# A decoder layer with three mixing branches: value weights split early, gate steps shared by two mLSTM units, three mLSTM operations on GpSimd

## Chip, cores and metric

One NeuronCore of a Trainium2 chip runs the whole layer. The metric is the device time in microseconds of one execution; lower is better. The kernel before takes 2176.12 us, the median of three runs (2176.08 to 2177.18).

## What is computed

The layer normalises x (1024 tokens of 1024 features), projects it, and runs three branches side by side: an mLSTM matrix memory (4 heads, keys of 128, values of 256, chunks of 128 tokens), causal differential attention, and cross attention into 256 memory tokens. Learned gates merge them; an MLP follows. The part that matters here, cut from the reference:

```
h = rms_norm(x, norm_mix_g[l])
mq, mk, mv, mi, mf, mo, dq, dk, dv, cq = jnp.split(h @ w_in[l], split_idx, axis=-1)
qk = jax.nn.silu(causal_depthwise_conv(jnp.concatenate([mq, mk], axis=-1), conv_w[l], conv_b[l]))
hm = mlstm_chunkwise(...)
y_m = jax.nn.sigmoid(mo) * rms_norm(hm, m_norm_g[l])
# mlstm_chunkwise, per chunk:
w_intra = jnp.exp(logd - m_loc[..., None])          # masked by causality
w_inter = jnp.exp(inter - m_loc)
s = jnp.einsum('bhjd,bhsd->bhjs', qq, kk) * w_intra
num = jnp.einsum('bhjs,bhsv->bhjv', s, vv) + w_inter[..., None] * jnp.einsum('bhjd,bhdv->bhjv', qq, C)
C_new = decay[..., None, None] * C + jnp.einsum('bhs,bhsd,bhsv->bhdv', w_s, kk, vv)
g_m, g_d, g_c = jnp.split(jax.nn.sigmoid(h @ w_gate[l] + b_gate[l]), N_BRANCH, axis=-1)
```

## The kernel before

Every fp32 matrix operand is held as two parts: ACT casts it to the high part (a CAST in the profile) and DVE subtracts that from the source to get the low part (a TENSOR_TENSOR or SCALAR_TENSOR_TENSOR from two inputs). `split`, `split2` and `splits` (L104 to L121, L247) do this, and `mm3` (L123) makes a product of two such operands by three matmuls. Nearly all of TensorE's matmuls have line L93.

Within a stage the code sets the order of the work by hand. `weave` (L608) runs a stream of steps, one product of an operand pair (three matmuls) at each, and issues items of other work when the stream has come to their position p. Instructions issued through `InOrder` (L58) or `pin` (L88), TensorE's among them, stay in that order on their engine; the others, GpSimd's in `branch_m` among them, are placed by the scheduler. Each engine works through its own queue in order; SP issues the loads and stores. L68 is the helper behind `InOrder`, so that many instructions have this line and are told apart by their tiles.

Three stages matter, one after the other.

`branch_c` (L440) is cross attention. Its stream has 64 query steps and then 32 gate steps (p from 65 to 96). Gate steps come from `gate_steps` (L579): a matrix of `h @ w_gate`, at the end of each 8 steps an activation on ACT into the tile gt and a store of gt by SP (L604, "gates<-gt"). The items are the scores, the probabilities (`probs` L502: RECIPROCAL and then the product cpe, on GpSimd for seven tiles and on DVE for the eighth), their transposes cpT and the value products sc<-cpT,mv.

`m_first` (L701) begins the mLSTM branch. `pieces` (L716) loads the first head's value weights (wmv3, tiles raw) and splits them into eight w tiles of 128x264; then eight value tiles (24 matmuls each) are made with them, of which va is the split result, and 32 gate steps follow. Beside this, at positions p of these 96 steps, `whole` (L773) makes four products hb on GpSimd (128x2048 each), `sums` (L778) four sums of each on DVE, and `low` (L785) splits them into sx; `raw`, `wsum` and `wsp` (L745 to L765) load, sum and split the output-gate weights into wo. Then come seven units of products of sums and weight sums, seven at a time, each in a PSUM bank of its own (bk). Two of the banks are those that the gate tiles use.

`branch_m` (L917) has eight units, head 3, 2, 1, 0 times the two halves of the sequence. Per unit the stream makes q and k (`f_tile`, two tiles of 8 steps) and, except for head 3, the values (`v_tile`); after the first unit's q and k it has 32 gate steps. `conv` (L972) makes the convolution and SiLU (tiles pre, cv, cth) and the operands qh and kh. The items of a unit are `inter` (L1002: wib, loaded, times q, gives qp), `decays` (L1035: ngb, loaded, plus the causal mask, then four exponentials on ACT), `krows` (transposes of k, scaled into ks), `scores` (k times q, times ngb, split into mpT), four times `chunk` (L1070: products with mpT, ks, qp and the state; the state C and its split Ch go on to the next chunk), and three times `final` (L1110: the output hS is scaled, transposed and gated). Their positions stand in the table at L1169 to L1184: kt for krows, st for scores, ch for the chunks, fi for the finals.

Of the kernel before, what the change touches and what calls it, by code (L numbers as in the profile page):

```python
# [10 lines left out]
F32 = mybir.dt.float32  # L11
F32R = mybir.dt.float32r
# [5 lines left out]
P = 128  # L18
# [54 lines left out]
class Layer:  # L73
# [366 lines left out]
    def branch_c(self, pool):  # L440
# [102 lines left out]
        for k in range(NK):  # L543
            add(41 + 2 * k + k // 2, self.gate_load)
        b4 = ((58, 64), (66, 69), (70, 74), (75, 79)), ((84, 87), (87, 90), (90, 93), (93, 96))
# [155 lines left out]
    def m_first(self, gp, wrp, sxp, wop, evp, pbk):  # L701
# [12 lines left out]
        wqk, wv = self.wqk, self.wv = {}, {}  # L714

        def pieces(d, hd, src, n, wait):  # L716

            d[hd] = []
            rq = []
            k = 0  # L720
            while k < NK or rq:
                while k < NK and len(rq) < wait:
                    raw = wrp.tile([P, 528], F32, tag="wraw", name=self.name("raw"))
                    S.dma_start(raw[:, 0 : 2 * n].rearrange("p (k n) -> p k n", k=2), src[:, k : k + 2, :])
                    rq.append(raw)
                    k += 2
                raw = rq.pop(0)
                for i in range(2):
                    t = self.wp.tile([P, 2, 264], F32R, tag="w", name=self.name("w"))
                    self.split2(t[:, 0, 0:n], t[:, 1, 0:n], raw[:, i * n : (i + 1) * n])  # L730
                    d[hd].append((t[:, 0, 0:n], t[:, 1, 0:n]))
                    yield

        for _ in pieces(wv, 3, a["wmv3"], 264, 4):
            pass
# [75 lines left out]
        def at(n, f):  # L811
            todo.setdefault(n, []).append(f)
# [13 lines left out]
        at(78, lambda: (wsum(2), sums(2)))  # L826
        at(82, lambda: (wsp(), raw(), wsum(3)))
        at(84, lambda: low(2))
        at(90, lambda: (wsp(), raw()))
# [24 lines left out]
        bank = [bank[0], b0[0], bank[1], b0[1]] + bank[2:]  # L854
# [3 lines left out]
        qk = pieces(wqk, 3, a["wmqk"][3], 256, 4)  # L858
# [58 lines left out]
    def branch_m(self, pool, tail):  # L917
# [84 lines left out]
        def inter(hd, hf, part=2):  # L1002
# [11 lines left out]
            V.tensor_mul(wib, wib, h["cv"][0])  # L1014
# [20 lines left out]
        def decays(hd, hf, part=2):  # L1035
# [10 lines left out]
            V.tensor_add(  # L1046
# [63 lines left out]
        def final(hd, hf, m):  # L1110
            h = H[hd, hf]
            hS, ss = h["hS"], h["ss"]
            if m == 0:
                for i in range(4):
                    self.pin(V.tensor_scalar_mul(hS[:, i], hS[:, i], ss[:, 4 + i : 5 + i]))
                return
# [19 lines left out]
        def stream():  # L1136
            for n in range(8):
# [7 lines left out]
                if n == 0:  # L1145
                    for _ in range(32):
                        next(filler)
                        yield
# [18 lines left out]
        for n in range(8):  # L1167
            hd, hf = heads[n // 2], n % 2
            if n == 0:  # L1169
# [854 lines left out]
    def run(self):  # L2024
        tc, nc = self.tc, self.nc
        with ExitStack() as ctx:
# [23 lines left out]
            with ExitStack() as c1:  # L2050
# [7 lines left out]
                with ExitStack() as c2:  # L2058
                    E2 = lambda *x, **k: c2.enter_context(tc.tile_pool(*x, **k))
                    kv = E2(name="kv", bufs=1)  # L2060
                    self.wp = E2(name="wp", bufs=4, side="right")
                    self.rp = E2(name="rp", bufs=5, side="right")
# [7 lines left out]
                    with tc.tile_pool(name="rpc", bufs=2) as self.grp, tc.tile_pool(name="pc", bufs=2) as pc, tc.tile_pool(name="pc1", bufs=1) as pc1, tc.tile_pool(name="pc3", bufs=3) as pc3, tc.tile_pool(name="pc4", bufs=8) as pc4, tc.tile_pool(name="wpc", bufs=8) as self.gwp:  # L2070
# [5 lines left out]
                        self.branch_c(T2())  # L2076
                with ExitStack() as c3:
                    E3 = lambda *x, **k: c3.enter_context(tc.tile_pool(*x, **k))
                    R3 = lambda n, k, **kk: Ring([E3(name=f"{n}{i}", bufs=1, **kk) for i in range(k)])
                    gm = E3(name="gm", bufs=1, side="right")  # L2080
                    self.wp = R3("wpa", 8, side="right")
                    with ExitStack() as c4:
                        E4 = lambda *x, **k: c4.enter_context(tc.tile_pool(*x, **k))
                        R4 = lambda n, k, **kk: Ring([E4(name=f"{n}{i}", bufs=1, **kk) for i in range(k)])
                        wrp = R4("wrm", 4, side="right")
# [4 lines left out]
                        self.m_first(gm, wrp, sxp, wop, evp, pbk)  # L2090
# [108 lines left out]
```

## Time and profile before

| | |
|---|---|
| median of three runs | 2176.12 us |
| the profiled execution, its time | 2179.45 us |
| its span, first to last instruction | 2177.7 us |
| busy: TensorE, DVE, ACT, GpSimd | 2145.4, 1444.7, 972.2, 620.0 us |
| share of the span | 99%, 66%, 45%, 28% |
| mean granted clock of TensorE | 0.995 |

Cross attention ends near 172 us of the span, `m_first` runs from there to 361.6, `branch_m` from there to about 625. PE is TensorE, POOL is GpSimd, PEld the weight loads of TensorE. A timeline joins instructions of one kind that follow each other; the time in square brackets is how long the engine stood before them, and on what. In the windows, PEclk is the granted clock of TensorE, where 1.00 is 2.4 GHz and 0.50 is 1.2 GHz. The end of a matmul is modelled, so the starts are what can be relied on. Spans on GpSimd are rough.

### The profile page before, as it was taken

Reading aid. Unit: us, or ns where it says so; the run is one execution under the profiler, and the core shown is the slowest. Engines: PE = TensorE matmul, PEld = TensorE weight load, DVE = VectorE, ACT = ScalarE, POOL = GpSimd, SP = SyncE. Lnnn points to the kernel's source line nnn. Section 1 sums busy time; section 2 is a strip of 40 time slices with the busy share of each in tenths; the row PEclk is TensorE's granted clock in tenths of the full one; section 3 lists DMA queues with packets and bytes.
Section 4 is the critical chain, followed back from the end, with each engine's and each line's share of the span. In section 5 each row is a group of like instructions: output and inputs, shape, how many; then the busy total and the mean of one; then the engine's idle time right before and its main releaser. Section 6 shows DMA issues by size and latency. Waiting matters only on the chain. (4 is left out here: it accounts for less than half of the span.)

```text
span 2177.7 us, 30462 instructions
## 1 busy us (share of the span) xinstructions
PE 2145.4 (99%) x11042; PEld 1850.7 (85%) x11042; DVE 1444.7 (66%) x2620; ACT 972.2 (45%) x1933; POOL 620.0 (28%) x833
## 2 busy tenths in 40 slices
PE   8998999999999999999999999999999999999998
PEld 7888788899989999999988888888778888788887
DVE  6446745767625888888864333553588778876678
ACT  7543334555534666666654120223433333543331
POOL 2213641000001111111100002202566666564444
PEclk9999999999999999999999999999999999999999
DMA  7022236331131111111125443435534454744442
GB/s 254 20 88 76 84 108 198 100 95 54 45 121 47 44 49 42 45 49 40 37 85 164 155 160 111 136 116 184 164 131 173 141 208 145 283 161 151 160 159 97
DMA packets 116100, 254.96 MB, mean 117 GB/s; under 512 B 11721, under 2 KB 20206, under 8 KB 113902
## 3 DMA queue, kind: packets, MB, share of 16 engines
q1 hardware_dynamic: 113646, 240.44, 33.8%
q10 hardware_dynamic: 2304, 12.58, 1.4%
q8 instruction: 87, 1.43, 0.3%
q14 instruction: 63, 0.52, 0.1%
HBM read 177.45 MB, written 71.34 MB: 114 GB/s over the span
## 5 line engine op out<-in xcount | busy, mean ns | idle before, releaser
L93 PE MATMUL mm<-w,hT 128*128 128x384 f32 (+3 forms) x2496 | 458.3, 331 | 6.7 <-DVE w L68 5.0
L68 POOL TENSOR_TENSOR wraw<-wraw 128x128 f32<-128x128 f32 x608 | 385.2, 658 | 231.1 <-DMA wraw<-in_wdown 122.2
L93 PEld LDWEIGHTS mm<-w,hT 128*128 128x128 f32 x2496 | 392.5, 190 | 19.5 <-DVE w L68 5.4
L93 PE MATMUL p<-xo,wo 128*128 128x512 f32 x1344 | 307.4, 390 | 3.4 <-DVE u L68 1.7
L93 PE MATMUL p<-xd,wo 128*128 128x512 f32 x1344 | 306.1, 389 | 0.8 <-DVE acc_xt L68 0.5
L93 PEld LDWEIGHTS p<-xo,wo 128*128 128x128 f32 x1344 | 251.6, 188 | 58.0 <-DVE u L68 3.0
L93 PEld LDWEIGHTS p<-xd,wo 128*128 128x128 f32 x1344 | 251.9, 188 | 54.8 <-DVE acc_xt L68 0.9
L93 PE MATMUL mm<-hT,w 128*128 128x512 f32 x1152 | 287.2, 397 | 0.2
L68 DVE TENSOR_TENSOR wo<-wraw,wo 128x896 fp32r<-128x896 f32 x153 | 186.0, 1225 | 140.3 <-ACT wo L68 138.4
L68 ACT CAST wo<-wraw 128x896 fp32r<-128x896 f32 x153 | 142.7, 943 | 297.9 <-POOL wraw L68 125.6
L93 PE MATMUL mm<-kt,w 128*128 128x512 f32 x1152 | 261.3, 389 | 0.0
L93 PEld LDWEIGHTS mm<-kt,w 128*128 128x128 f32 x1152 | 216.2, 188 | 44.9
L93 PEld LDWEIGHTS mm<-hT,w 128*128 128x128 f32 x1152 | 209.6, 188 | 42.6 <-ACT pre L980 0.5
L68 ACT ACTIVATE dpe<-sc,dst,drr 128x256 f32<-128x256 f32 (+7 forms) x128 | 106.6, 833 | 73.6 <-DVE dst L68 72.6
L117 ACT CAST w<-raw 128x256 fp32r<-128x256 f32 (+1 forms) x80 | 51.4, 662 | 126.4 <-PE mm L93 101.1
L68 DVE CUSTOM_DVE_ANT_0 sc<-sc,tmask 128x256 f32<-128x256 f32 (+7 forms) x128 | 97.2, 759 | 5.3 <-PE sc L93 4.3
L68 DVE TENSOR_TENSOR w<-raw,w 128x384 fp32r<-128x384 f32 (+3 forms) x128 | 76.6, 615 | 34.1 <-ACT w L68 34.0
L118 DVE TENSOR_TENSOR w<-raw,w 128x256 fp32r<-128x256 f32 (+1 forms) x80 | 61.7, 786 | 39.7 <-ACT w L117 39.6
L141 POOL TENSOR_SCALAR dso<-dso 128x4 f32<-128x4 f32 x16 | 3.4, 210 | 295.4 <-DVE dso L68 295.4
L93 PE MATMUL bk<-sx,wo 128*128 128x512 f32 x336 | 85.6, 390 | 1.5 <-ACT gt L68 1.5
L93 PE MATMUL mm<-mh,w 128*128 128x512 f32 x256 | 79.0, 389 | 0.0
L93 PEld LDWEIGHTS bk<-sx,wo 128*128 128x128 f32 x336 | 63.0, 188 | 15.0 <-ACT gt L68 1.9
(344 smaller groups left out, 3224.4 us busy)
## 6 DMA issues: line engine op xcount, KB each, us to landing
wraw<-in_wup SPq DMA_DIRECT2D x64, 256.0 KB, 3.3
r_d<-xts SPq DMA_DIRECT2D x16, 1024.0 KB, 4.3
xd<-r_d SPq DMA_DIRECT2D x16, 1024.0 KB, 5.4
wraw<-in_wdown SPq DMA_DIRECT2D x64, 256.0 KB, 5.3
raw<-in_wd SPq DMA_DIRECT2D x32, 384.0 KB, 3.2
kraw<-y SPq DMA_DIRECT2D x24, 512.0 KB, 4.6
gl<-gates SPq DMA_DIRECT2D x48, 256.0 KB, 2.7
r_d<-rq ACTq DMA_DIRECT2D x16, 768.0 KB, 3.3
```

Of the source, the lines that this page charges most:

```text
L68: return self.tc.keep_in_program_order(f(*a, **k))
L93: self.pin(self.nc.tensor.matmul(out, l, r, start=start, stop=stop))
L117: nc.scalar.copy(hi, src)
L118: nc.vector.tensor_sub(lo, src, f32(hi))
L141: g.tensor_scalar(r, ss, 1.0 / width, EPS, op0=ALU.mult, op1=ALU.add)
```

## The change

It has three parts. **Early splits:** at p = 72 of `branch_c` two pools that are no longer used are closed and those of the value weights opened; the loads of wmv3 start there, and its eight splits are issued at p = 78 to 92. The pool of the gate tiles and gate bias in `m_first` moves to the other side of the memory, so that the gate bias load now comes behind the last cross-attention matmuls. **Gate steps and positions:** of the 32 gate steps after the first unit's q and k, 16 stay there and 16 come after the second unit's, and the positions of the units' items are new; in `m_first` sums(2), low(2) and the third wsp come earlier, and the second of the two banks that gate tiles use takes the seventh product instead of the fourth. **GpSimd:** in `branch_m` the mask addition on ngb, the product wib, and the scaling of hS (four DVE operations of 128x256 before, now one product of 128x1024) run on GpSimd.

The diff, cut to its core:

```diff
-    def branch_c(self, pool):
+    def branch_c(self, pool, room):
...
+        def begin():
+            room()
+            self.early = self.pieces(self.wv, 3, self.a["wmv3"], 264, 4)
+
+        add(72, begin)
+        for p in (78, 80, 82, 84, 86, 88, 90, 92):
+            add(p, lambda: next(self.early))
...
-        for _ in pieces(wv, 3, a["wmv3"], 264, 4):
+        for _ in self.early:
             pass
...
-        at(78, lambda: (wsum(2), sums(2)))
+        at(76, lambda: (wsum(2), sums(2)))
         at(82, lambda: (wsp(), raw(), wsum(3)))
-        at(84, lambda: low(2))
-        at(90, lambda: (wsp(), raw()))
+        at(80, lambda: low(2))
+        at(88, lambda: (wsp(), raw()))
...
-        bank = [bank[0], b0[0], bank[1], b0[1]] + bank[2:]
+        bank = [bank[0], b0[0]] + bank[1:5] + [b0[1], bank[5]]
...
-            V.tensor_mul(wib, wib, h["cv"][0])
+            G.tensor_mul(wib, wib, h["cv"][0])
...
-            V.tensor_add(
+            nc.gpsimd.tensor_add(
                 ngb.rearrange("p (t j) -> p t j", t=4), ngb.rearrange("p (t j) -> p t j", t=4),
                 self.tmaskT.unsqueeze(1).broadcast_to([P, 4, P]),
             )
...
             if m == 0:
-                for i in range(4):
-                    self.pin(V.tensor_scalar_mul(hS[:, i], hS[:, i], ss[:, 4 + i : 5 + i]))
+                self.pin(G.tensor_mul(hS, hS, ss[:, 4:8].unsqueeze(2).broadcast_to([P, 4, 256])))
                 return
...
-                if n == 0:
-                    for _ in range(32):
+                if n < 2:
+                    for _ in range(16):
                         next(filler)
                         yield
...
-                kt, st, ch, fi = 32, 35, (39, 43, 47, 51), (62, 72, 78)
+                kt, st, ch, fi = 29, 34, (38, 42, 46, 50), (55, 63, 68)
             elif n == 1:
-                add(62, inter, hd, hf)
-                add(70, decays, hd, hf)
-                kt, st, ch, fi = 77, 82, (85, 91, 98, 104), (112, 118, 123)
+                add(50, inter, hd, hf)
+                add(56, decays, hd, hf)
+                kt, st, ch, fi = 60, 66, (72, 77, 82, 88), (97, 107, 113)
...
-                ch, fi = (e + 7, e + 11, e + 15, e + 21), (e + 33, e + 44, e + 50)
+                ch, fi = (e + 7, e + 11, e + 15, e + 21), (e + 32, e + 45, e + 51)
...
+                    def room():
+                        cr.close()
+                        R = lambda c, n, k: Ring([c.enter_context(tc.tile_pool(name=f"{n}{i}", bufs=1, side="right")) for i in range(k)])
+                        self.wp = R(cw, "wpa", 8)
+                        self.wrp = R(cq, "wrm", 4)
...
-                    gm = E3(name="gm", bufs=1, side="right")
-                    self.wp = R3("wpa", 8, side="right")
+                    c3.push(cw)
+                    gm = E3(name="gm", bufs=1)
```

How the instructions move is shown at three places. The first is DVE in cross attention, round the eighth cpe product (cpT are low parts of transposed probabilities, yc copies of the branch's output). Before:

```order
L68 TENSOR_TENSOR cpT_1372<-tp_1367,cpT_1372 128x512
L68 TENSOR_TENSOR cpT_1383<-tp_1378,cpT_1383 128x512
L68 RECIPROCAL cmx_1314<-cmx_1314 128x4
L68 TENSOR_TENSOR cpe_1340<-cpe_1340,cmx_1314 128x1024
L68 COPY yc_1410<-sc_1397 128x512
L68 COPY yc_1413<-sc_1397 128x512
```

Now:

```order
L68 TENSOR_TENSOR cpT_1410<-tp_1405,cpT_1410 128x512
L68 TENSOR_TENSOR cpT_1421<-tp_1416,cpT_1421 128x512
L68 TENSOR_TENSOR w_1438<-raw_1430,w_1438 128x264
L68 RECIPROCAL cmx_1314<-cmx_1314 128x4
L68 TENSOR_TENSOR cpe_1378<-cpe_1378,cmx_1314 128x1024
L68 COPY yc_1459<-sc_1446 128x512
L68 COPY yc_1462<-sc_1446 128x512
L68 TENSOR_TENSOR w_1471<-raw_1430,w_1471 128x264
L68 TENSOR_TENSOR w_1481<-raw_1432,w_1481 128x264
L68 TENSOR_TENSOR w_1490<-raw_1432,w_1490 128x264
```

The subtraction that makes the low part of the first value-weight tile, w_1438, stands ahead of the RECIPROCAL and the cpe product, and three more follow the copies yc.

The second is ACT at the end of the gate steps of `m_first` (gt are the gate activations after 8, 16, 24 and 32 steps; sx_2143 and sx_2121 are the third sum's high parts in the two kernels, wo the output-gate weights). Before:

```order
L68 CAST sx_2056<-hb_1764 128x4x512
L68 ACTIVATE gt_2071<-mm_2039,dv 128x512
L68 CAST wo_2087<-wraw_2021 128x7x128
L68 ACTIVATE gt_2118<-mm_2080,dv 128x512
L68 CAST wo_2128<-wraw_2023 128x7x128
L68 CAST sx_2143<-hb_2013 128x4x512
L68 ACTIVATE gt_2158<-mm_2121,dv 128x512
L68 CAST wo_2168<-wraw_2025 128x7x128
L68 ACTIVATE gt_2191<-mm_2161,dv 128x512
```

Now:

```order
L68 CAST sx_2056<-hb_1764 128x4x512
L68 ACTIVATE gt_2071<-mm_2039,dv 128x512
L68 CAST wo_2087<-wraw_2021 128x7x128
L68 ACTIVATE gt_2118<-mm_2080,dv 128x512
L68 CAST sx_2121<-hb_2013 128x4x512
L68 CAST wo_2131<-wraw_2023 128x7x128
L68 ACTIVATE gt_2158<-mm_2124,dv 128x512
L68 CAST wo_2161<-wraw_2025 128x7x128
L68 ACTIVATE gt_2191<-mm_2166,dv 128x512
```

The cast of sx stands ahead of the second wo cast instead of behind it, and the third gt behind both; on SP the order of loads and stores is as before, a load of wraw ahead of each store of gt, and that ahead of the third store refills the buffer that the second wo is split from.

The third is the start of `branch_m`, first on ACT (cth, qh and qp are of the first unit's q, kh and ks of its k, gt are gate activations, the first of which frees the bank of the tile after next). Before:

```order
L991 ACTIVATE cth_3382<-cv_3377 128x512
L1053 ACTIVATE ngb_3328<-ngb_3328,g_col 128x128 x4
L120 ACTIVATE qh_3385<-cv_3377 128x512
L120 ACTIVATE qp_3410<-wib_3330 128x512
L603 ACTIVATE gt_3504<-mm_3471,dv 128x512
L991 ACTIVATE cth_3433<-cv_3428 128x512
L117 CAST kh_3436<-cv_3428 128x512
L603 ACTIVATE gt_3540<-mm_3507,dv 128x512
```

Now:

```order
L1062 ACTIVATE ngb_3328<-ngb_3328,g_col 128x128 x4
L1000 ACTIVATE cth_3382<-cv_3377 128x512
L120 ACTIVATE qh_3385<-cv_3377 128x512
L1000 ACTIVATE cth_3433<-cv_3428 128x512
L120 ACTIVATE qp_3410<-wib_3330 128x512
L612 ACTIVATE gt_3504<-mm_3471,dv 128x512
L117 CAST kh_3436<-cv_3428 128x512
L253 ACTIVATE ks_3533<-tp_3528,g_col 128x128 x4
L612 ACTIVATE gt_3554<-mm_3507,dv 128x512
```

The exponentials of ngb stand ahead of the activation of q, and qp and the first gt behind that of k. On GpSimd the moved operations come in this order, where ngb_3328 and wib_3330 are of the first unit, ngb_3804 and wib_3770 of the second, ngb_4184 of the third (before, GpSimd had only the hss operations here):

```order
L1055 TENSOR_TENSOR ngb_3328<-ngb_3328,tmaskT 128x512
L1055 TENSOR_TENSOR ngb_3804<-ngb_3804,tmaskT 128x512
L1023 TENSOR_TENSOR wib_3330<-wib_3330,cv_3377 128x512
L1055 TENSOR_TENSOR ngb_4184<-ngb_4184,tmaskT 128x512
L1023 TENSOR_TENSOR wib_3770<-wib_3770,cv_3629 128x512
L141 TENSOR_SCALAR hss_3600<-hss_3600 128x4
L142 TENSOR_TENSOR hss_3600<-hss_3600,mhalf 128x4
L1123 TENSOR_TENSOR hS_3599<-hS_3599,hss_3600 128x1024
```

The second unit's mask addition stands between the first unit's mask addition and its product wib, which on DVE came before it.

## Rows read from the trace of the kernel before

**Rows 1.** The page, section 1: busy us (share of the span) x instructions of each engine.
```profile
PE 2145.4 (99%) x11042; PEld 1850.7 (85%) x11042; DVE 1444.7 (66%) x2620; ACT 972.2 (45%) x1933; POOL 620.0 (28%) x833
```

**Rows 2.** The list of TensorE's waits: line waited for: us in total, times, longest.
```profile
PE bk L93 <- ACT gt L68: 1.7, 2, 1.5
...
PE sc L93 <- DVE Ch L118: 0.6, 2, 0.4
```

**Rows 3.** Timeline of TensorE, 170 to 204: start, us, what, [idle before <-releaser].
```profile
169.66 2.26 PE L93 MATMUL sc<-cpT,mv 128*128 128x512 f32 x9
...
178.93 24.58 PE L93 MATMUL mm<-w,hT 128*128 128x264 f32 x188 [4.03 <-DVE w L68]
...
182.81 20.70 PE L93 MATMUL mm<-w,hT 128*128 128x264 f32 x168
203.35 0.86 PE L93 MATMUL mm<-hT,gws 128*128 128x512 f32 x3
```

**Rows 4.** Timeline of DVE, 169 to 184.
```profile
173.22 7.71 DVE L68 TENSOR_TENSOR w<-raw,w 128x264 fp32r<-128x264 f32 x8
```

**Rows 5.** Timelines of GpSimd, DVE and TensorE in cross attention, 130 to 153.
```profile
135.68 1.89 POOL L507 TENSOR_TENSOR cpe<-cpe,cmx 128x1024 f32<-128x1024 f32 x1 [9.30 <-DVE cmx L68]
...
142.07 1.22 DVE L68 TENSOR_TENSOR cpe<-cpe,cmx 128x1024 f32<-128x1024 f32 x1
...
148.77 0.60 PE L96 MATMUL tp<-ident,cpe 128*128 128x128 f32 x4
```

**Rows 6.** Timeline of TensorE, 224 to 233.
```profile
229.34 1.65 PE L93 MATMUL bk<-sx,wo 128*128 128x512 f32 x6 [1.50 <-ACT gt L68]
```

**Rows 7.** Timelines of ACT and DVE, 213 to 232.
```profile
225.46 0.67 ACT L68 ACTIVATE gt<-mm,dv 128x512 f32<-128x512 f32 x1
226.04 0.93 ACT L68 CAST wo<-wraw 128x896 fp32r<-128x896 f32 x1
228.59 0.69 ACT L68 ACTIVATE gt<-mm,dv 128x512 f32<-128x512 f32 x1 [1.63 <-DMA gates<-gt]
...
227.79 1.34 DVE L68 TENSOR_TENSOR wo<-wraw,wo 128x896 fp32r<-128x896 f32 x1
```

**Rows 8.** Timelines of DVE and TensorE, 413 to 439.
```profile
414.72 1.14 DVE L1115 TENSOR_SCALAR hS<-hS,hss 128x256 f32<-128x256 f32 x4
...
430.57 0.50 PE L93 MATMUL sc<-va,mpT 128*128 128x258 f32 x2 [1.60 <-ACT mpT L117]
431.74 0.58 PE L93 MATMUL sc<-va,mpT 128*128 128x258 f32 x1 [0.66 <-DVE mpT L118]
...
432.76 4.04 PE L93 MATMUL mm<-w,hT 128*128 128x256 f32 x18
```

**Rows 9.** Windows: length, PE, PEld, DVE, ACT, POOL busy (x), PEclk, DMA.
```profile
42.00:48.00 6.00, 4.06 (x19) 3.26 (x20) 6.00 (x10) 4.55 (x8) 0.00 (x0) 0.79 0.50 150
413.00:432.00 19.00, 16.27 (x91) 13.58 (x90) 19.00 (x42) 11.70 (x27) 0.00 (x0) 0.98 0.38 126
431.00:438.00 7.00, 6.34 (x30) 6.26 (x30) 4.54 (x13) 3.38 (x9) 0.00 (x0) 0.51 0.26 76
```

**Rows 10.** Timelines of TensorE and DVE, 360 to 394.
```profile
361.56 22.81 PE L93 MATMUL mm<-hT,w 128*128 128x512 f32 x96
...
384.56 2.32 PE L93 MATMUL mm<-hT,w 128*128 128x512 f32 x9
...
382.08 0.69 DVE L1046 TENSOR_TENSOR ngb<-ngb,tmaskT 128x512 f32<-128x512 f32 x1 [0.17 <-DMA ngb<-g_dng]
```

**Rows 11.** Groups by line on GpSimd: shapes xcount | busy us, mean ns | idle.
```profile
L68 POOL TENSOR_TENSOR xts<-rq 128x512 f32<-128x512 f32 x15 | 19.6, 1305 | 60.2 <-ACT rq L68 60.2
...
L507 POOL TENSOR_TENSOR cpe<-cpe,cmx 128x1024 f32<-128x1024 f32 x7 | 13.5, 1933 | 15.5 <-DVE cmx L68 15.5
```

**Rows 12.** Timelines of GpSimd and DVE, 203 to 216.
```profile
205.20 4.62 POOL L68 TENSOR_TENSOR hb<-hT 128x2048 f32<-128x2048 f32 x1 [26.62 <-DVE sx L68]
...
205.76 6.20 DVE L68 TENSOR_TENSOR sx<-hb,sx 128x2048 fp32r<-128x2048 f32 x1 [0.17 <-ACT sx L68]
```

More of the change, by code (lines that the diff above doesn't have):

```diff
@@ L544, in branch_c @@
             add(41 + 2 * k + k // 2, self.gate_load)
+        self.wqk, self.wv = {}, {}
+        def begin():
[4 more added lines that the diff above has]
+            add(p, lambda: next(self.early))
         b4 = ((58, 64), (66, 69), (70, 74), (75, 79)), ((84, 87), (87, 90), (90, 93), (93, 96))
@@ L699, in m_gates2, with pieces, m_first @@
         self.pin(self.nc.scalar.copy(self.gcol, ps2[:, 0 : 3 * W]))
-    def m_first(self, gp, wrp, sxp, wop, evp, pbk):
+    def pieces(self, d, hd, src, n, wait):
+        d[hd] = []
+        rq, wrp = [], self.wrp
+        k = 0
+        while k < NK or rq:
+            while k < NK and len(rq) < wait:
+                raw = wrp.tile([P, 528], F32, tag="wraw", name=self.name("raw"))
+                self.S.dma_start(raw[:, 0 : 2 * n].rearrange("p (k n) -> p k n", k=2), src[:, k : k + 2, :])
+                rq.append(raw)
+                k += 2
+            raw = rq.pop(0)
+            for i in range(2):
+                t = self.wp.tile([P, 2, 264], F32R, tag="w", name=self.name("w"))
+                self.split2(t[:, 0, 0:n], t[:, 1, 0:n], raw[:, i * n : (i + 1) * n])
+                d[hd].append((t[:, 0, 0:n], t[:, 1, 0:n]))
+                yield
+    def m_first(self, gp, sxp, wop, evp, pbk):
         nc, a = self.nc, self.a
@@ L713, in m_first @@
         va = self.va = [gp.tile([P, 2, 258], F32R, name=f"va{t}") for t in range(8)]
[L714 to L732, printed above, removed]
-        for _ in pieces(wv, 3, a["wmv3"], 264, 4):
+        wqk, wv, wrp = self.wqk, self.wv, self.wrp
+        for _ in self.early:
             pass
@@ L857, in m_first @@
         at(1, lambda: low(3))
-        qk = pieces(wqk, 3, a["wmqk"][3], 256, 4)
+        qk = self.pieces(wqk, 3, a["wmqk"][3], 256, 4)
         for i, n in enumerate((-5, -5, -4, -4, -3, -3, -2, -2)):
@@ L2060, in run @@
                     kv = E2(name="kv", bufs=1)
-                    self.wp = E2(name="wp", bufs=4, side="right")
-                    self.rp = E2(name="rp", bufs=5, side="right")
+                    cr = ExitStack()
+                    self.wp = cr.enter_context(tc.tile_pool(name="wp", bufs=4, side="right"))
+                    self.rp = cr.enter_context(tc.tile_pool(name="rp", bufs=5, side="right"))
+                    cw, cq = ExitStack(), ExitStack()
+                    def room():
[3 more added lines that the diff above has]
+                        self.wrp = R(cq, "wrm", 4)
                     with tc.tile_pool(name="ptmp", bufs=1) as tmp0, tc.tile_pool(name="ptmp2", bufs=2) as tmp, tc.tile_pool(name="ptmp8", bufs=8) as tmp8:
@@ L2075, in run @@
                         self.gpool = T2()
-                        self.branch_c(T2())
+                        self.branch_c(T2(), room)
                 with ExitStack() as c3:
@@ L2084, in run @@
                         R4 = lambda n, k, **kk: Ring([E4(name=f"{n}{i}", bufs=1, **kk) for i in range(k)])
-                        wrp = R4("wrm", 4, side="right")
+                        c4.push(cq)
                         sxp = [E4(name=f"sxp{i}", bufs=1) for i in range(4)]
@@ L2089, in run @@
                         pbk = E4(name="pbk", bufs=1, space=PSUM)
-                        self.m_first(gm, wrp, sxp, wop, evp, pbk)
+                        self.m_first(gm, sxp, wop, evp, pbk)
                     self.psc = E1(name="psc2", bufs=2, space=PSUM)
```

## Prediction, made before the changed kernel was run

> **What bounds the kernel now.** I read the page's busy times first: TensorE is busy 99% of the span [rows 1]. No other engine can be the bound over the whole program, and the change removes no matmul, so all it can win is time in which TensorE stands, and time in which it runs at the lower clock after standing. Next I read the list of TensorE's waits, to see which of them lie where the change works, then the timelines round each, and last the clock of those stretches. Three places come out.
>
> At the start of the first mLSTM stage, `m_first` (place A), the last matmuls of cross attention end at 169.66 + 2.26 = 171.92 us and the gate tiles begin at 203.35 [rows 3]. In between lie eight value tiles of 24 matmuls. From 182.81 on they run undisturbed, 168 matmuls in 203.35 - 182.81 = 20.54 us, 122.3 ns each [rows 3], so all 192 need 23.5 us. They got 31.4. Some 8.0 us are lost, 4.03 of them in one wait at 178.93. The reader should see why: the eight subtractions that make the low parts of the value weights occupy DVE for 7.71 us from 173.22 on [rows 4].
>
> At the switch from gate tiles to output-gate products (place B) TensorE waits twice for a gate activation, 1.7 us together, the longer one at 229.34 [rows 2, 6].
>
> In the second mLSTM unit (place C) it waits 1.60 and 0.66 us for the two halves of mpT, because DVE has no idle time at all from 413 to 432 [rows 8, 9]. Then it runs at half clock, 1.2 GHz of 2.4, from 431 to 438 [rows 9]: 18 matmuls of 256 columns from 432.76 on take 4.04 us [rows 8], 224 ns each against some 122 of 264 columns at place A, so somewhat over 40% of those 7 us, some 3.0, are lost too. C costs 5.3 us.
>
> **The change, part by part.** Durations are from one profiled execution of 2179.45 us (span 2177.7, the rest lies around it); it is 0.15% over the median of 2176.12. I add up differences in that execution and take them off the median.
>
> *Early splits: -8.0 us.* The sixteen casts and subtractions, with their four loads, move into cross attention, onto ACT, DVE and SP. Eight subtractions at about 0.4 us find room on DVE there. One spot is tight. The two products hb for the later sums no longer wait for buffers of cross attention, so GpSimd should run them right after its last cpe product, which ended at 135.68 + 1.89 = 137.57 [rows 5]. At about 4.6 us each [rows 12] they hold GpSimd until about 146.8. The first moved subtraction now stands on DVE ahead of the RECIPROCAL and the cpe product, which needs 1.22 us [rows 5]. If GpSimd holds it until 146.8, then 0.42 + 0.17 + 1.22 end at 148.6, and TensorE takes the result at 148.77 [rows 5]: hidden, with 0.2 to spare. Without that cover one transpose waits up to 2 us. The gate bias load, now behind the last cross-attention matmuls on SP with the gate-weight loads after it, ends well before the first tile's results need it two tiles later. Bounds -6 (a late cpe) to -8.0; I take -8.0, since the row of the cpe leaves room.
>
> *First-stage order: +1.4 us.* On ACT the cast of sx now comes ahead of the second wo cast, and the third gate activation behind both. It ran at 225.46, right after sx, and the wo cast that followed took 0.93 [rows 7]; the activation moves by about 0.84, and the wait of 0.2 behind it becomes about 1.05. The product that uses the last bank moves from fourth to seventh place, from which three places of 0.71 us are gained (96 matmuls in 22.81 us are 0.71 for three [rows 10]). But the last gate activation also shares its one buffer with the third: it started at 228.59, when that store had landed, 2.46 us after the third activation's end at 226.13 [rows 7]. In the changed order SP holds a weight load ahead of that store, and the load waits for the second wo's low part, which now ends at 227.79 + 1.34 = 229.13 [rows 7]. So: store at 229.5, landing about 231.9, activation done at 232.6. The seventh product could start at 227.05 + 5 x 0.71 = 230.6. It waits 2.0. Together 3.05 against 1.7. Bounds: -0.5, if the load gets out of the way, +2.5 with a late landing.
>
> *Sixteen gate steps before and sixteen after the first half-head: -4.8 us.* The second unit's convolutions now run in the first unit's stretch, and 16 steps of 0.71 us stand ahead of its key rows. The scores no longer have convolutions, qh and wib of two units between them and mpT on DVE. I take 5.3 off and leave 0.5 for the closer spacing; bounds -5.3 and -3.
>
> *Start of the mLSTM units: +1.5 us.* Mask and inter product move to GpSimd, which runs them in the order mask 0, mask 1, inter 0. On DVE mask 1 sat at 382.08, having waited for its transfer [rows 10], and inter 0 had been done before it. Now inter 0 stands behind that transfer. With 1.3 us for a product of this shape on GpSimd [rows 11]: 382.1 + 1.3 + 1.3 = 384.7. On ACT qp follows, and the gate activation behind qp frees the bank for the next tile: 0.67 each, as the gate takes it [rows 7], so 386.0. That tile could start at 384.56 [rows 10]. TensorE waits 1.5 (a wait of 0.6 for the key transposes lies inside it). Bounds 0, if the transfer lands earlier, and 2.5, with a DVE subtraction of 0.7 ahead of each GpSimd product.
>
> *GpSimd in the other units: +0.3 us.* Per unit DVE loses 0.69 + 0.69 (one of them in [rows 10]) + 1.14 for the output scaling [rows 8], and GpSimd gains 1.3 + 1.3 + 1.93 = 4.5, by its products of 128x512 and 128x1024 [rows 11]. The rows show what this can do: a DVE subtraction started at 205.76, 0.56 us into a GpSimd product of 4.62, and took 6.20, which is until 2.1 us after that product's end [rows 12]. In the units the only chain with no slack is the state's low part Ch, 0.6 us in two waits [rows 2]. A relieved DVE may save these; one hS product of 1.93 that blocks Ch at both places costs 3.9. Bounds -0.6 and +3.9; I take +0.3, nearer to the rows of today's waits. The Trainium skill says the same more sharply ("SBUF — State Buffer", section "SBUF: two separate sides"): a DVE operation with two SBUF inputs and a GpSimd operation hold a common pair of ports in turn, the loser standing for the whole instruction. The row at 205.76 agrees. By that rule at its hardest the sum would not be +0.3 but the third rival's.
>
> Sum: -8.0 + 1.4 - 4.8 + 1.5 + 0.3 = -9.6, so 2166.5 us.
>
> **The rivals.**
> *1. The new waits at B lower the clock.* At 42 to 48 TensorE was idle 1.94 us of 6 and the mean clock fell to 0.79 [rows 9]; at B today's 1.7 us brought no such loss, and 3.05 lies above both. The lower clock cost 3.0 at C. With it, and the start of the units at its bound of +2.5, the sum is -5.6: 2170.5. For: the waits follow from the orders. Against: they are two, with 3.5 us of work between.
> *2. All goes clean.* The store at B slips past the load, the mask transfers land early, and Ch no longer waits: -8.0 - 1.7 - 5.3 - 0.6 = -15.6, 2160.5. For: the transfers vary, and DVE is freer. Against: GpSimd's order and SP's order are fixed.
> *3. GpSimd and DVE block each other; slower than before.* If each of the eight units loses to DVE what GpSimd holds, 4.5 us, less the 2.5 that DVE no longer does, DVE falls behind by 2.0 us a unit, 16 us. This decides where DVE has no idle time, as from 413 to 432 [rows 9]: there each microsecond reaches mpT or Ch and so TensorE. The sum becomes -9.9 + 16 = +6, 2182. It turns slower than before from about 1.25 us a unit on. For: the 6.20 us row. Against: the second unit is spread out, and the other units show 0.6 us of such waits in all.
> *4. The early split does only half.* If the four loads or the split's buffers are held until cross attention releases its last pool, the casts slip past its end and only some 4 us of A go: 2170.5. Against: the new pools are opened at step 72 of 96.
>
> **How the numbers follow.** The forecast has 0.52, rival 1 0.18, rival 2 0.15, rival 3 0.07, rival 4 0.08. The time is the forecast's, 2166.5. Its own bounds reach from about 2163 to 2169. To leave out no more than two in ten the range takes in rival 2 and most of rivals 1 and 4: 2160.5 to 2171.5. A measurement of this kernel tells about 0.2%, 4.4 us, from no change. Forecast and rival 2 are faster by more than that, and so are three quarters of rivals 1 and 4: 0.86. The rest of these and a part of rival 3 are within it: 0.09. The rest of rival 3 is slower: 0.05.
>
> **What would show it.** Right: no wait of TensorE for w at the first value tile and full clock there, the gate tiles beginning some 23.5 us after the last cross-attention matmuls; no wait for mpT in the second unit; two waits for gt at B, the longer before the seventh product; one wait of about 1.5 us, or two smaller ones, 23 us into the mLSTM units. Wrong: a wait of cross attention for cpe or cpT near 149; half clock at B; waits for Ch or mpT of over 1 us in several units, with DVE instructions there far longer than before. If the waits for Ch and mpT over the last six units grow beyond 4 us, or place A keeps more than 2 us, the forecast fails.

## The result and the profile after

The changed kernel takes 2179.57 us in the median of 20 runs (2175.07 to 2184.01), the kernel before 2176.16 in 20 runs beside them (2174.21 to 2177.62). The ratio is 1.0016, 95% interval 1.0009 to 1.0023: 3.4 us longer by the medians, where 9.6 us less was forecast. The profiled execution took 2178.97 us (span 2177.2). That of before stood 3.3 us over its median, this one 0.6 under, which hides the loss when the two spans are compared.

The page of the changed kernel, busy time of each engine:

```profile
PE 2145.2 (99%) x11042; PEld 1847.9 (85%) x11042; DVE 1442.1 (66%) x2572; ACT 971.2 (45%) x1933; POOL 656.0 (30%) x857
```

Beside [rows 1] DVE has lost 48 instructions and almost no time. The list of what TensorE waited for, over the whole program:

```profile
PE bk L93 <- ACT gt L68: 3.5, 2, 3.1
...
PE sc L93 <- DVE Ch L118: 2.5, 6, 0.9
...
PE sc L93 <- ACT Ch L117: 2.3, 3, 1.2
PE tp L96 <- POOL ngb L1055: 1.5, 1, 1.5
...
PE tp L96 <- POOL hS L1123: 1.2, 2, 1.0
```

The waits for mpT are gone. Those for gt and Ch [rows 2] have doubled and grown eightfold, and two waits for GpSimd are new.

**Place A gave the time that was forecast.** The timeline of TensorE there:

```profile
169.90 2.96 PE L93 MATMUL sc<-cpT,mv 128*128 128x512 f32 x12
172.70 23.46 PE L93 MATMUL mm<-w,hT 128*128 128x264 f32 x192
...
196.00 22.56 PE L93 MATMUL mm<-hT,gws 128*128 128x512 f32 x96
```

All 192 value matmuls run without a wait, and the gate tiles begin at 196.00 instead of 203.35 [rows 3], although the last cross-attention matmuls began 0.94 us later: 8.3 us won. But the loss had another cause than the prediction read out of [rows 4]. GpSimd and DVE in the kernel before:

```profile
169.35 9.22 POOL L68 TENSOR_TENSOR hb<-hT 128x2048 f32<-128x2048 f32 x2 [31.78 <-PE mm L93]
...
174.13 4.74 DVE L68 TENSOR_TENSOR w<-raw,w 128x264 fp32r<-128x264 f32 x1
```

Six of the eight subtractions take 0.42 us each. The first took 0.99 and the second 4.74, until GpSimd's second product hb had ended at 178.57, and TensorE's wait of 4.03 us ended behind it. Over the whole kernel before, 146 DVE instructions run more than 0.15 us longer than the median of their kind and shape, 54 us together, and every one of them overlaps a GpSimd instruction. In the changed kernel the two hb products run earlier, and the first moved subtraction meets them; GpSimd, DVE and TensorE:

```profile
138.49 9.18 POOL L68 TENSOR_TENSOR hb<-hT 128x2048 f32<-128x2048 f32 x2
...
144.52 3.43 DVE L68 TENSOR_TENSOR w<-raw,w 128x264 fp32r<-128x264 f32 x1 [1.62 <-ACT w L68]
...
149.71 0.60 PE L96 MATMUL tp<-ident,cpe 128*128 128x128 f32 x4
```

It ends at 147.95, the cpe product behind it at 149.31, and the transposes of cpe start at 149.71 without a wait. Here the prediction had reckoned with the block, and it stayed hidden.

**Place B lost more.** Timelines of TensorE, ACT and SP:

```profile
219.72 0.96 PE L93 MATMUL bk<-hT,wo 128*128 128x512 f32 x3 [0.46 <-ACT gt L68]
...
226.50 0.97 PE L93 MATMUL bk<-sx,wo 128*128 128x512 f32 x3 [3.09 <-ACT gt L68]
...
225.76 0.69 ACT L68 ACTIVATE gt<-mm,dv 128x512 f32<-128x512 f32 x1 [5.27 <-DMA gates<-gt]
...
222.25 0.42 SPq L613 DMA_DIRECT2D gates<-gt  x1
```

The long wait stands before the seventh product, as the prediction had it, but is 3.09 us, not 2.0. The store of gt starts behind the weight load at 222.25, and the next activation, which needs its buffer, at 225.76, some 3.5 later, where a landing 2.4 after the issue had been taken.

**TensorE's pace fell, with no wait and no lower clock.** Starts of TensorE's products after B, first of the changed kernel, then of the one before; between the rows of one kernel lie 21 matmuls of 512 columns:

```profile
231.45 0.85 PE L93 MATMUL bk<-sx,wo 128*128 128x512 f32 x3
...
236.30 0.85 PE L93 MATMUL bk<-sx,wo 128*128 128x512 f32 x3
```

```profile
203.35 21.95 PE L93 MATMUL mm<-hT,gws 128*128 128x512 f32 x96
...
236.28 0.84 PE L93 MATMUL bk<-sx,wo 128*128 128x512 f32 x3
...
241.04 0.84 PE L93 MATMUL bk<-sx,wo 128*128 128x512 f32 x3
```

These are 4.85 against 4.76 us, 231 ns a matmul against 226.7. The 96 gate matmuls take 22.56 against 21.95 us. By 361 us the lead over the kernel before has shrunk from 4.8 to 2.6 us this way.

**In the mLSTM units GpSimd took back what DVE was given.** At their start, timelines of GpSimd, DVE and TensorE:

```profile
379.04 1.36 POOL L1055 TENSOR_TENSOR ngb<-ngb,tmaskT 128x512 f32<-128x512 f32 x1 [3.71 <-DMA ngb<-g_dng]
...
379.19 1.76 DVE L1001 SCALAR_TENSOR_TENSOR cv<-cth,cv 128x512 f32<-128x512 f32 x1
...
381.16 0.63 PE L96 MATMUL tp<-ident,cv 128*128 128x128 f32 x4 [1.52 <-POOL ngb L1055]
```

The product cv on DVE, 0.69 us elsewhere, starts 0.15 us into the second unit's mask addition and takes 1.76; the transposes of that cv wait 1.52. In the second unit, GpSimd, ACT, DVE and TensorE:

```profile
424.37 1.30 POOL L1055 TENSOR_TENSOR ngb<-ngb,tmaskT 128x512 f32<-128x512 f32 x1 [11.73 <-DMA ngb<-g_dng]
...
425.70 1.28 ACT L1062 ACTIVATE ngb<-ngb,g_col 128x128 f32<-128x128 f32 x4 [3.68 <-POOL ngb L1055]
426.88 0.39 ACT L117 CAST Ch<-C 128x258 fp32r<-128x258 f32 x1
...
422.59 0.47 DVE L1103 SCALAR_TENSOR_TENSOR C<-C,g_dec,sc 128x258 f32<-128x258 f32 x1
...
427.31 0.43 DVE L118 TENSOR_TENSOR Ch<-C,Ch 128x258 fp32r<-128x258 f32 x1 [3.58 <-ACT Ch L117]
...
427.33 0.96 PE L93 MATMUL sc<-Ch,qp 128*128 128x258 f32 x3 [0.64 <-ACT Ch L117]
```

Here DVE is not held. ACT's queue stands 3.68 us for the masked ngb, and the cast of the state Ch, whose input C DVE had finished at 422.59 + 0.47 = 423.06, stands behind it. Of the 3.68 us, 2.35 pass before the mask's load has landed and GpSimd starts at 424.37. So only a part is GpSimd's: with the mask on DVE (e2 below) ACT stands at the same place for 2.52 us, behind a load that comes late too:

```profile
422.98 1.29 ACT L1062 ACTIVATE ngb<-ngb,g_col 128x128 f32<-128x128 f32 x4 [2.52 <-DVE ngb L1055]
```

From 362 to 640 ACT stands for masks seven times, 17.2 us, in the changed kernel, and four times, 6.2 us, in e2. Three units later, GpSimd and DVE:

```profile
523.77 1.41 POOL L1023 TENSOR_TENSOR wib<-wib,cv 128x512 f32<-128x512 f32 x1 [3.96 <-DVE cv L1001]
...
523.95 1.25 DVE L1111 TENSOR_TENSOR den<-den,g_col 128x1 f32<-128x1 f32 x1
```

A product of one column, 0.15 us in the kernel before, takes 1.25, until GpSimd's product of 128x512 ends. Of the 24 masks, wib and hS products on GpSimd, 17 lengthened a DVE instruction so (by over 0.15 us against the median of its kind and shape), by 17.1 us in all; before, none was lengthened between 360 and 626. The moved work had cost DVE 20.1 us there. So by this count the relief for DVE was some 3 us; the page's totals, 1444.7 and 1442.1, differ by 2.6.

### The profile page after: what moved, and what is told of

The parts are those of the page before. It is cut to its first block, busy times and chain, and to the rows that moved or that the text cites. A ratio compares the mean times of both kernels' runs of the same rounds, so it can differ in the third digit from the quotient of the medians.

```text
span 2177.2 us, 30443 instructions
## 1 busy us (share of the span) xinstructions
PE 2145.2 (99%) x11042; PEld 1847.9 (85%) x11042; DVE 1442.1 (66%) x2572; ACT 971.2 (45%) x1933; POOL 656.0 (30%) x857
## 5 line engine op out<-in xcount | busy, mean ns | idle before, releaser
L118 DVE TENSOR_TENSOR w<-raw,w 128x256 fp32r<-128x256 f32 (+1 forms) x80 | 67.1, 859 | 42.7 <-ACT w L117 42.7
```

Source lines behind the costliest of these rows:

```text
L118: nc.vector.tensor_sub(lo, src, f32(hi))
```

## The experiments

Every edit is made to the changed kernel. Times are from five rounds each; a difference "to before" is the ratio's distance from 1 times 2176 us.

**e1: is it the alignment of the gate bias to 64 bytes?** The smallest tile in the pool that moved sides has 32 bytes a partition, so the place of what follows it depends on that length.

```diff
-        gb = gp.tile([P, 8], F32, name="gbias")
+        gb = gp.tile([P, 16], F32, name="gbias")[:, 0:8]
```

> The changed kernel with one edit: the gate bias tile is 64 bytes per partition instead of 32, so that every tile allocated behind it starts 32 bytes further. In the changed kernel 512-column matmuls take 231 to 235 ns from the gate tiles on to the end of the first mLSTM stage, where they took 226.7 before, at full clock in both; the tiles that moved start at an odd multiple of 32 bytes. Theory A (the start addresses of the streamed operand and of the next weights, compared modulo 64 bytes, set the pace): 226.7 ns again in that stage, 3.0 to 3.6 us less than the changed kernel, so about 0 us against the kernel before. Rival (the pace differs by chance between executions, or by what else runs): 231 ns again and the same +3.4 us against before.

Measured: 2177.15 us, ratio 1.0014 (1.0005 to 1.0023). The gate matmuls still take 22.56 us, so 64 bytes are not it.

**e2: how much do the three GpSimd operations cost together?**

```diff
-            nc.gpsimd.tensor_add(
+            V.tensor_add(
...
-            G.tensor_mul(wib, wib, h["cv"][0])
+            V.tensor_mul(wib, wib, h["cv"][0])
...
-                self.pin(G.tensor_mul(hS, hS, ss[:, 4:8].unsqueeze(2).broadcast_to([P, 4, 256])))
+                for i in range(4):
+                    self.pin(V.tensor_scalar_mul(hS[:, i], hS[:, i], ss[:, 4 + i : 5 + i]))
```

> The changed kernel with the mask addition, the inter product and the output scaling back on DVE; positions, early splits and orders stay. Theory Q (GpSimd is late: the exponentials of ngb stand on ACT until its addition is done, and hold the casts of the state behind them): TensorE's waits for Ch (4.8 us), for ngb before the first key transposes (1.5) and for hS (1.2) go, and the half clock near 525 with them: 7 to 9 us less than the changed kernel, 4 to 5 us faster than before. Rival P (the new positions are too tight, whichever engine works): at least 4 us of the waits for Ch stay, and the time is within 3 us of the changed kernel's.

Measured: 2170.88 us, ratio 0.998 (0.9971 to 0.9989), -4.4 us to before and 7.8 less than the changed kernel. No DVE instruction is lengthened between 360 and 626, and TensorE waits there for little:

```profile
PE sc L93 <- DVE Ch L118: 1.2, 4, 0.3
PE tp L96 <- issue: 0.5, 1, 0.5
PE sc L93 <- DVE mpT L118: 0.2, 1, 0.2
```

**e3: is it the mask alone?** Only its first edit of e2 (ngb on DVE).

> The changed kernel with the mask addition alone back on DVE; inter product and output scaling stay on GpSimd. Theory Q: the waits for Ch fall to 1 us or less in all, that for ngb goes, those for hS (1.2 us) stay: 5 to 7 us less than the changed kernel. Rival L (GpSimd's operations hold DVE's two-input subtractions, wherever they stand): the inter product and the scaling go on doing so, half of the 4.8 us for Ch or more stays, and 1 to 3 us are gained.

Measured: 2177.83 us, ratio 1.0014 (1.0005 to 1.0023): no gain. The waits for Ch fall from 4.8 to 1.5 us, so the mask on GpSimd does lengthen them. But the start of the units got worse, as in e9 below, with a wait of 3.07 before the key transposes. The theory that the mask is the cost fell: with the other two on GpSimd it is worth 0.4 us.

**e4 and e10: the early splits alone.** All of e2, and the sums, banks and positions of the kernel before (of the positions' table one changed line of five is shown); gbias at 64 bytes in e4 and 256 in e10.

```diff
-        at(76, lambda: (wsum(2), sums(2)))
+        at(78, lambda: (wsum(2), sums(2)))
-        at(80, lambda: low(2))
+        at(84, lambda: low(2))
-        at(88, lambda: (wsp(), raw()))
+        at(90, lambda: (wsp(), raw()))
-        bank = [bank[0], b0[0]] + bank[1:5] + [b0[1], bank[5]]
+        bank = [bank[0], b0[0], bank[1], b0[1]] + bank[2:]
...
-                if n < 2:
-                    for _ in range(16):
+                if n == 0:
+                    for _ in range(32):
...
-                kt, st, ch, fi = 29, 34, (38, 42, 46, 50), (55, 63, 68)
+                kt, st, ch, fi = 32, 35, (39, 43, 47, 51), (62, 72, 78)
```

> Of the change only the early splits of the first value weights (with the pools that they need), and the 64-byte gate bias tile; orders, positions and engines are those of the kernel before. Theory: the 8 us at the start of the first mLSTM stage are gained and nothing is given back: 7.5 to 8.5 us faster than before. Rival (the clock or a later wait takes part of it back, since all that follows starts earlier): 3 to 6 us faster. Without the padding theory A says 3.3 us of it would be lost.

> Of the change only the early splits, with the 256-byte gate bias tile; orders, positions and engines as before. Theory: the 7.8 us of the run with 64 bytes and the 3.3 us of pace add up: 10.5 to 11.5 us faster than before. Against the run that has the new positions as well (10.4 to 11.1 us faster) this prices the positions: the prediction gave them 4.8 us, so this one should then be 5.5 to 6.5 us faster only; if the positions are worth nothing on DVE, both are equal within 1 us.

Measured: e4 2167.10 us, ratio 0.9966 (0.9953 to 0.9978); e10 2164.69 us, ratio 0.9953 (0.994 to 0.9967), -10.2 us. Place A's 8.3 lies inside e10's interval; no more than that can be said of the 2 us between them. Both keep the waits for mpT; TensorE and two windows (length, PE, PEld, DVE, ACT, POOL, clock, DMA) of e10:

```profile
421.64 0.51 PE L93 MATMUL sc<-va,mpT 128*128 128x258 f32 x2 [1.60 <-ACT mpT L117]
422.81 0.39 PE L93 MATMUL sc<-va,mpT 128*128 128x258 f32 x1 [0.66 <-DVE mpT L118]
```

```profile
416.00:424.00 8.00, 5.32 (x42) 4.73 (x41) 8.00 (x16) 3.43 (x6) 0.00 (x0) 1.00 0.29 100
424.00:432.00 8.00, 8.00 (x70) 8.00 (x69) 5.17 (x18) 5.28 (x19) 0.00 (x0) 1.00 0.22 66
```

The same two waits as in [rows 8], and the clock stays at 2.4 GHz. In e4 it fell (0.79 from 422 to 430). So these waits do not bring the half clock of [rows 9] every time. How often it comes in the kernel before is not shown: of its 78 executions in the rounds of e1 to e12, 18 have the profiled one's mean granted clock, 0.995, and 60 have 0.996 or 0.997.

**e5: the same tile at 256 bytes.** `[P, 16]` of e1 becomes `[P, 64]`.

> The changed kernel with the gate bias tile made 256 bytes per partition, 224 more than now, so that the tiles behind it start again at the same place modulo 512 bytes as the normalised input hT, as in the kernel before. Theory A2 (a 512-column matmul takes 226.7 ns where its streamed operand and the weights loaded for the next one start at the same address modulo 512, and some 231 to 234 elsewhere; 64 bytes were too coarse a measure): 227 ns again in the first mLSTM stage, 3 to 3.6 us less than the changed kernel, so -0.5 to +0.5 us against before. Rival (the pace of that stage hangs on something else, as the run with 64 bytes suggests): 231 ns as there, and +2.2 to +3.4 us against before.

Measured: 2175.97 us, ratio 1.0006 (0.9998 to 1.0015), 2.2 us less than the changed kernel. The old pace is back:

```profile
194.68 21.95 PE L93 MATMUL mm<-hT,gws 128*128 128x512 f32 x96
...
236.46 0.84 PE L93 MATMUL bk<-sx,wo 128*128 128x512 f32 x3
...
241.22 0.84 PE L93 MATMUL bk<-sx,wo 128*128 128x512 f32 x3
```

**e6, e7, e9: one operation on GpSimd at a time.** e2 without its third edit (scaling, e6), without its first (mask, e7), without its second (inter product, e9).

> The changed kernel with the mask addition and the inter product on DVE and only the output scaling on GpSimd; to be held against the run with all three on DVE, 4.05 us faster than before. Theory Q (what hurts is what stands in front of ACT's queue, above all the mask addition): the waits for hS, 1.2 and 0.4 us, are all that comes back: 2 to 3 us faster than before. Rival L (any GpSimd operation holds DVE): a third or more of the 7.5 us comes back, 1.5 us faster than before or less.

> The changed kernel with the inter product and the output scaling on DVE and only the mask addition on GpSimd. Theory Q: most of the 7.5 us comes back with it, 4 us at least: 0 to 3 us slower than before, with waits for Ch after ACT stood for ngb. Rival L: it has a share of a third, 2.5 us: 1 to 2 us faster than before.

> The changed kernel with the mask addition and the output scaling on DVE and only the inter product on GpSimd. The run with inter product and scaling on GpSimd was 7 us slower than the one with none there, the one with the scaling alone 0, the one with the mask alone 1.7 us slower. Theory I (the inter product is the costly one: it starts when the convolution of q ends, the moment at which DVE has the low part of qh, the state and den to do, and its result stands in front of ACT's queue): 5 us slower at least than with none there, so 1 to 4 us slower than before, with DVE operations lengthened during each of the eight products. Rival (it was the two together): 2 to 3 us slower than with none there, 1 to 2 us faster than before.

Measured: e6 2170.88 us, ratio 0.9984 (0.9975 to 0.9993); e7 2172.57 us, 0.9989 (0.998 to 0.9997); e9 2176.50 us, 1.0007 (0.9998 to 1.0016). Against e2 that is +0.9, +2.0 and +5.9 us, of which the first two are within the intervals. For e9 theory I came out. Theory Q came out for neither e6 nor e7: e6 is 3.5 us faster than before where it said 2 to 3, and e7 is not slower than before but 2.4 us faster. The three prices add up to 8.8 us and the three operations together cost 7.8, but the mask on top of the other two cost 0.4 (e3), so they do not simply add. The scaling also lengthens DVE instructions (four, by 4.7 us in all), but those are splits of weights with time to spare. The inter product in e9, timelines of GpSimd, DVE and TensorE:

```profile
375.01 1.69 POOL L1023 TENSOR_TENSOR wib<-wib,cv 128x512 f32<-128x512 f32 x1 [41.23 <-DVE cv L1001]
...
375.42 1.30 DVE L988 COPY pre<-pre 128x3 f32<-128x3 f32 x1
...
378.40 0.70 DVE L1055 TENSOR_TENSOR ngb<-ngb,tmaskT 128x512 f32<-128x512 f32 x1 [1.67 <-DMA ngb<-g_dng]
...
382.62 1.09 PE L96 MATMUL tp<-ident,cv 128*128 128x128 f32 x4 [2.77 <-issue]
```

A copy of three columns is held until wib ends, DVE then stands for the second unit's mask transfer, with the key convolution behind it, and TensorE waits 2.77 us. In e2 qh, qp and the last sum of that convolution stand ahead of the mask on DVE. So a part of e9's price may be the order that the scheduler chose once wib was on GpSimd; no run separates it from the block. After that its clock falls:

```profile
380.00:386.00 6.00, 3.38 (x11) 2.89 (x12) 3.49 (x9) 2.39 (x6) 0.00 (x0) 0.72 0.15 44
```

**e8, e11, e12: the order at place B.** e11 is e2 with 256 bytes of gbias; e8 also has the sums, splits and banks of the kernel before (the first eight lines of the diff of e10), and e12 only its sums and splits (the first six), with the new order of banks.

> The changed kernel with all three operations on DVE, the 256-byte gate bias tile, and the order of sums, splits and banks at the end of the gate steps as before; the early splits and the new positions stay. If the three causes (GpSimd 7.5 us, pace 3.3, the waits for gt at the switch 1.9 more than before) add up: 9 us faster than before, 12.5 less than the changed kernel. If pace and waits are not causes of their own: 4 to 6 us faster.

> The changed kernel with all three operations on DVE and the 256-byte gate bias tile; the new order of sums, splits and banks at the end of the gate steps stays. Against the run that has the old order as well, this prices the order: the profile shows 1.9 us more of waits for gt with the new one, so 8.5 to 9.5 us faster than before if nothing else hangs on it; as fast as with the old order (10.4 to 11.1 us) if the later waits absorb it.

> The fastest version so far (early splits, new positions, all three operations on DVE, 256-byte gate bias tile, old order of sums and splits: 10.4 us faster than before) with the new order of banks put back: the second bank of the gate tiles is used by the seventh product instead of the fourth. With the old order of sums and splits the third gate activation, its store and the fourth are early again, and the seventh product starts 2.1 us after the place of the fourth: the longer wait for gt, 1.5 us, should go and the short one of 0.2 to 0.4 stay: 11.5 to 12.5 us faster than before. If the banks were what made the changed kernel's wait of 3.1 us, it is slower than the fastest version by 1 us or more.

Measured: e8 2163.63 us, ratio 0.9952 (0.994 to 0.9965); e11 2167.01 us, 0.9967 (0.9955 to 0.998); e12 2164.03 us, 0.9943 (0.9929 to 0.9956). e8 against e11: the new order at B costs 3.3 us. In e11 the waits of 1.07 and 2.88 us are followed by low clock, here in the window behind them:

```profile
226.00:232.00 6.00, 6.00 (x21) 4.85 (x20) 3.69 (x2) 2.74 (x2) 3.45 (x7) 0.74 0.24 87
```

That window is at 0.72 to 0.78 in five of the nine profiled kernels with the new order (e1, e2, e5, e9, e11) and at 1.00 in the other four (the changed kernel, e3, e6, e7). With the old order (e8) the waits are 0.24 and 1.49 and the clock stays at 1.00. In e12 the only wait at B is this:

```profile
218.22 0.96 PE L93 MATMUL bk<-hT,wo 128*128 128x512 f32 x3 [0.23 <-ACT gt L68]
```

By the waits the move of the bank was good, and the moved sums and splits spoiled it. e12 beats both kernels, by 12.4 us the one before (interval 9.6 to 15.5); its gain over e8 is within the intervals, and only the missing wait of 1.49 us speaks for it.

## Why the prediction was wrong

By ratios, each run held against the next, the +3.4 us divide so: early splits -10.2 (e10), positions -0.2 (e8 against e10), order at B +3.3 (e11 against e8), pace +2.8 (e2 against e11), GpSimd +7.8 (the changed kernel against e2); sum +3.5. Against the forecast's -9.6 the miss is 13.1: GpSimd 6.0, positions 4.6, pace 2.8, order at B 1.9, less 2.2 that the early splits gave more. That the sum comes out proves nothing, as the steps lead from the kernel before to the changed one. Each difference is uncertain by 2.5 to 4 us, from the two intervals, so the trace has to carry the smaller ones. Other runs give one check: e2 against e4 prices positions and order at B together at +3.0, where these steps give +3.1.

*Early splits, -8.0: the size was right, the cause misread.* The waits for w went, the pace there is 23.46 us for 192 matmuls, and nothing waits near 149 us for the late cpe. But the 7.71 us of [rows 4] were not eight subtractions' work. Two of them were held by GpSimd's hb products, 4.9 us together, which is the block that decided the last terms below, in the rows of the kernel before. The change took both the splits and the hb products away from there; whether moving the hb products alone would have been enough, no run shows.

*First-stage order, +1.4: mechanism right, size too small.* The place and the cause of the long wait were those named, a store behind a weight load behind the second wo's split. The store's buffer came free some 3.5 us after its issue instead of 2.4, and the waits grew from 1.7 to 3.55 us. On top came rival 1's lower clock in about half of the profiles: 0.26 of 6 us in e11, 1.6 us. 1.9 and half of 1.6 make 2.7; the runs say 3.3.

*Sixteen gate steps before and after, -4.8: wrong, it won nothing that the runs can tell from zero (-0.2).* The waits for mpT went as said. But the 3.0 us for the half clock were taken from one execution which stood 3.3 us over its median, and e10 shows the same waits without it. The other 2.3 us came back as new waits: in e8 TensorE waits 3.5 us from 362 to 640 (1.5 before the first key transposes, 2.0 for Ch), in e10 3.1. That the profiled execution stood above its median was in the prediction; that the half clock might be why was not drawn from it, and no run shows that it was.

*Start of the mLSTM units, +1.5: the size came out by luck, the way did not.* The wait is 1.52 us, but before the key transposes, because in the key's convolution DVE's copy of three columns and its cv were held by the two mask additions, 2.2 us together, and not for qp and the gate bank. The positions have a part in it: with all three operations on DVE the wait there is 0.5 us in e2, 1.5 in e8 and 1.8 in e12.

*GpSimd in the other units, +0.3: the step that failed most.* Its value was taken from the waits of the kernel before; the row that showed the price, 6.20 us for a DVE subtraction beside GpSimd's hb [rows 12], was read as a risk for hS and Ch alone. Together the two GpSimd terms were +1.8, with +6.4 as their upper bound, and measured +7.8. Of the signs that the prediction named for its failure one was there, DVE instructions far longer than before. The other was not reached: of the 4.8 us of waits for Ch 2.7 lie in the last six units, where 4 were named, and one wait alone is over 1 us. In the profile TensorE's waits from 362 to 640 are 7.5 us against 1.9 in e2, and the clock fell once (0.68 from 524 to 528). This is rival 3's block, at half its price of 16, but not its sum: DVE did not fall behind by 2.0 us a unit, it was busy some 3 us less in all, and by the rows above TensorE paid at the few places where it waited for a held instruction. With it came what no rival had, ACT's queue standing longer for a mask that GpSimd makes, with the state's cast behind; the mask alone on GpSimd (e7), with the DVE instructions that it holds, cost 2.0 us, within the intervals. The Trainium skill states the blocking as a rule ("SBUF — State Buffer", section "SBUF: two separate sides": of a GpSimd instruction that reads SBUF and a DVE instruction with two SBUF inputs or in a two-port mode, whichever starts first keeps the common ports for its whole instruction, and the other stands). The rows agree: den from 0.15 to 1.25 us, the copy of three columns from 0.16 to 1.30, each until GpSimd's product ends.

*Not in the sum: pace, +2.8.* The prediction treated the move of a pool to the other side of the memory as a matter of when a load can start. e1 and e5 differ in the length of one 32-byte tile only, and the pace with it.

Of the rivals, 2 and 4 were not seen; 1 came in part of the executions; 3's block decided the sign, with a chance of 0.07. Its argument "against", that the units show little waiting today, says what slack there was before and not what the blocking would take.

## What to carry to other kernels

Work moved from DVE to GpSimd relieves DVE only by what GpSimd does not block: count each GpSimd instruction as up to its own length on whatever short DVE instruction meets it, and look which queue (here ACT's) will stand for its result with other work behind. Look for this price in the trace at hand first: before a row of several instructions is read as work, hold the length of each against the median of its kind. When a pool is moved, compare the start-to-start time of undisturbed matmuls before and after it, as waits and clock say nothing there. Before a clock loss in one profile is booked as a gain, hold that execution's time against the median.

## What was not expected of the hardware

At the full granted clock a 512-column matmul took 226.7 ns in the kernel before, in e5 and in e8 to e12 but for e9 (21 in 4.76 us), and 231 ns for the products and 233 ns for the gate tiles in the changed kernel, e1 to e4, e6, e7 and e9 (21 products in 4.85 us; gate tiles from 196.00 to 218.40). What goes with it in six of these kernels (before, changed, e1, e2, e5, e10), by the addresses that the built programs give the tiles, is the distance between the start of the streamed operand and the start of the next matmul's weights: over some 20,000 matmuls the median from start to start was 227 ns where it is a multiple of 512 bytes, and 231 to 234 at every other distance. That is a sorting of the matmuls by address, not an experiment of its own; what the runs show is that the length of one tile sets the pace: the changed kernel and e5, e2 and e11, e4 and e10 differ in that alone and are 2.2 to 2.8 us apart. Why it is so stays open. The Trainium skill says ("TensorE: Matmul & The Clock Gate", section "Step-by-step: what each phase is for") that the next weights load over a port of their own and take nothing from the running matmul; if the sorting names the cause, that holds only for some placements here.

The lower clock did not follow from the length of a wait alone: after waits of about 3 us at B the granted clock of the stretch from 226 to 232 was 0.72 to 0.78 in five kernels and 1.00 in four with nearly the same wait. Each has one profile, so whether it differs between kernels or between executions of one is not shown.
